# Later gates, unsplit value products, wider down chunks and a merge whose state-space branch runs one chunk behind, in a two-layer diffusion block on one Trainium2 core

## The chip, the core and the metric

The program runs on one core of a Trainium2 chip. TensorE (PE in the rows; its weight loads are PEld) multiplies matrices into PSUM, VectorE (DVE) and ScalarE (ACT) work on SBUF and PSUM, and SyncE (SP) issues nearly all loads. Each engine runs its own instructions in a fixed order and waits at semaphores for the others. The metric is the time of one execution on the device in microseconds (us), as the median of a few runs.

## The reference

```python
for l in range(2):                       # 256 context + 256 latent tokens, width 1024, FFN width 2816
    x  = ffn_half(x,  ml[0:3], g[0], ffn1)          # x + 0.5*gate*(silu(h@wg)*(h@wu))@wd
    xc = ffn_half(xc, mc[0:3], g[0], ffn1)          # the same weights for the context stream
    u, gq, gk, gv, nq, nk, nv, gates = split_in(modulate(rmsnorm(x)) @ w_in)
    y_ssm = s5_mixer(...)                           # state space, gelu, then t * sigmoid(t @ w_glu)
    y_gqa = window_gqa_latent(...)                  # 8 heads of 64, 2 key heads, sink logit
    y_na  = neighborhood_attn_latent(...)           # 8 heads, local window, relative bias
    m = sig(g_s)*(y_ssm@w_p_ssm) + sig(g_a)*(y_gqa@w_p_gqa) + sig(g_n)*(y_na@w_p_na)
    x = x + ml[5] * (m @ w_out)
    # the context stream goes through the same mixers and merge in layer 0 only
    x  = ffn_half(x, ml[6:9], g[2], ffn2)           # context too in layer 0 only
return rmsnorm(x, final_g)
```

All of it is float32.

## The kernel before

Activations lie transposed: eight chunks of 128 channels by 512 columns, context in columns 0 to 255 and latent in 256 to 511. A weight chunk is loaded into `raw`, ScalarE rounds it to `whi`, VectorE keeps the rest as `wlo` (`wload`, L73 to L80, three buffers of each in a pool that all weights share), and one product is three matmuls: `whi` with the rounded activation, `whi` with its rest, `wlo` with the rounded activation (`mm3`, L82 to L85). Those three lines stand in nearly every row.

A half-step FFN (`ffn`, L388) makes 22 hidden chunks (`mid`) in two halves of eleven and after each half sums them down (`down`, L406): eight output chunks `pd` of 33 matmuls. The first half runs over all 512 columns. The second runs over the context's 256 columns for all eight chunks and then, with the weights loaded again, over the latent's 256; under the latter the next stage's norm of the context is threaded (`then`, a generator that is advanced once a chunk from the third on). That is so in three of the four FFNs; the last one has the latent alone. At the end the next stage begins with products of the context's half (`by_stream`, tiles `pbs`) while the latent's norm is finished.

The mixer (`mixer`, L707) projects with `proj` (tiles `pp`), and in four rounds does one chunk of window attention (two heads) and one of neighbourhood attention. `attend` (L804) makes scores `sc`, softmax on VectorE and ScalarE, transposes `pt`, copies `ptb`, and in `values` (L797) the products `po`: for each key block j and each of two heads a matmul that fills half of the array's columns. Between the calls `fill` computes some of the 24 merge gates (`gate`, 24 matmuls into `pp`, a tanh into `th`) early and parks them in HBM: all of branch 2 from chunk 1 on in layer 0, of branches 1 and 2 in layer 1 (`ahead`). After the last attention come the gates 0, 1, 2 of chunk 0 (L994).

The merge splits the eleven chunks of branch outputs into `yh` and `yl`, runs the state-space unit's gated product (`pgl`, with gelu before and tanh behind), and then goes through eight output chunks, each with three branches (`pbr`: 9, 12 and 12 matmuls) whose weights are three loads of 384, 512 and 512 columns, each times its gate. Then `w_out` (`pwo`). In layer 1 all this is done for the latent alone, over 256 columns.

The order on every engine is made by a scheduler from the program order, the dependences and the free buffers; `tc.issue_after(x)` keeps what it encloses behind instruction x in that order.

Of the kernel before, what the change touches and what calls it, by code (L numbers as in the profile page):

```python
# [10 lines left out]
F32 = mybir.dt.float32  # L11
# [16 lines left out]
def body(tc, A):  # L28
# [359 lines left out]
    def ffn(tp, l, n, streams, hook, mids=None, before=None, then=None):  # L388
        i = 2 * n
        both = len(streams) == 2  # L390
        c0 = HALF * streams[0]
        early = []

        def unit(f, j):
            w, ps = early.pop() if early else wload(A["up"][l, n, f, j], 1024), bank("pgu")
            for k in range(KC):
                mm_k(ps[:, :T - c0], w, k, c0, T)
            hook(0.01 * (T - c0))
            return ps

        def up(f, *done):
            mids[f] = mid_tiles(tp)
            pg, pu = [*done, *(unit(f, j) for j in range(len(done), 2))]
            gate_up(tp, mids[f], pg, pu, c0, T)

        def down(half, a, b, between=None):  # L406
            N = b - a
            for m in range(KC):
                if between and m >= 2:
                    next(between, None)  # L410
                ps = bank("pd")
# [295 lines left out]
    def mixer(l):  # L707
# [89 lines left out]
        def values(nk_, ptb, vt, out):  # L797
            po = pa.tile([128, T], F32, name="po", tag="po")
            for j in range(nk_):
                for hf, r in enumerate(halves):  # L800
                    PE.matmul(po[r, :HALF], vt[:, j, r], ptb[hf][:, j], start=j == 0, stop=j == nk_ - 1)  # L801
            S.copy(out, po[:, :HALF])

        def attend(K, Q, vt, out, heads, bias):  # L804

            for s in streams:
# [3 lines left out]
                for b in range(2):  # L810
                    q0 = HALF * s + 128 * b
                    ps = [pa.tile([128, T], F32, name="sc", tag="sc", bufs=2) for hf in range(2)]
                    for hf in range(2):
                        for j in range(2):
                            PE.matmul(ps[hf][:, :128 * nk_], Q[:, hf, q0:q0 + 128], K[:, hf, j, :128 * nk_], start=j == 0, stop=j == 1)  # L815
# [183 lines left out]
        yh = gp.tile([128, 11, T], F32R, name="yh")  # L999
        yl = gp.tile([128, 11, T], F32R, name="yl")  # L1000
        nat = lambda x: x.rearrange("p (x t) -> p x t", t=8)
        ty = [yP[:, c, :, x0:].rearrange("p t x -> p x t") for c in range(3)]
        S.activation(yP[:, :, :, x0:].rearrange("p c t x -> p (c t) x"), yP[:, :, :, x0:].rearrange("p c t x -> p (c t) x"),
                     AF.Gelu_apprx_tanh)
        for c in range(3):
            split(nat(yh[:, c, c0:]), nat(yl[:, c, c0:]), ty[c])
        pgs = []
        for c in range(3):
            wh, wl = wload(A["wglu"][l, c], 384)
            ps = bank("pgl")  # L1010
            for k in range(3):
                w = slice(128 * k, 128 * k + 128)
                mm3(ps[:, :N], wh[:, w], wl[:, w], yh[:, k, c0:], yl[:, k, c0:], k == 0, k == 2)
            pgs.append(ps)
        for c in range(3):
            g = pgs[c][:, :N]
            S.activation(g, g, AF.Tanh, scale=0.5)
            V.scalar_tensor_tensor(ty[c], nat(g), 1.0, ty[c], op0=ALU.add, op1=ALU.mult)
            glu_last = split(nat(yh[:, c, c0:]), nat(yl[:, c, c0:]), ty[c], scale=0.5)
        for src, o in ((gq, 3), (nq, 7)):  # L1020
            for c in range(4):
                split(yh[:, o + c, c0:], yl[:, o + c, c0:], src[:, c, c0:])
        mh = gp.tile([128, KC, T], F32R, name="mgh")
        ml = gp.tile([128, KC, T], F32R, name="mgl")
        spans = ((0, 3), (3, 7), (7, 11))
        later = Filler([], 0.34)
        if l == 0:
# [4 lines left out]
            def ada_late():  # L1032
                for j in range(40, 64):
                    junk = p3.tile([128, D], F32, name="ajunk", tag="ajunk", bufs=1)
                    ada_chunk(rw[:, j % 2], sb, junk, 0, j)
                    if j % 8 == 7:
                        ada_bias(0, j // 8)
                    yield 2.4
            anchor[0] = glu_last
            later.gens.append([ada_late(), 0])  # L1040
        for m in range(KC):
            acc = gp.tile([128, T], F32, name="macc", tag="macc")
            for b, (k0, k1) in enumerate(spans):
                j = 3 * m + b
                th = ths[b] if m == 0 else gate_back(j) if j in ahead else gate(j)
                wh, wl = wload(A["wp"][l, m][:, 128 * k0:128 * k1], 128 * (k1 - k0))
                pp = p3.tile([128, T], F32, name="pbr", tag="pbr")
                for k in range(k0, k1):
                    w = slice(128 * (k - k0), 128 * (k - k0) + 128)
                    mm3(pp[:, :N], wh[:, w], wl[:, w], yh[:, k, c0:], yl[:, k, c0:], k == k0, k == k1 - 1)  # L1050
                if b == 0:
                    V.scalar_tensor_tensor(acc[:, :N], th[:, :N], 1.0, pp[:, :N], op0=ALU.add, op1=ALU.mult)
                else:
                    V.scalar_tensor_tensor(th[:, :N], th[:, :N], 1.0, pp[:, :N], op0=ALU.add, op1=ALU.mult)
                    V.tensor_add(acc[:, :N], acc[:, :N], th[:, :N])
                if m:
                    later(0.01 * N + 0.00125 * N * (k1 - k0))
            split(mh[:, m, c0:], ml[:, m, c0:], acc[:, :N])
# [4 lines left out]
        for s in streams:  # L1063
            a, b = HALF * s, HALF * s + HALF
            ctx_norm = norm(l, 2, 0, 2) if s and not last else iter(())
            for m in range(KC):
                if m >= 2:
                    next(ctx_norm, None)
                wh, wl = wload(A["wout"][l, m], 1024)
                ps = bank("pwo")  # L1070
                for k in range(KC):
                    w = slice(128 * k, 128 * k + 128)
                    mm3(ps[:, :HALF], wh[:, w], wl[:, w], mh[:, k, a:b], ml[:, k, a:b], k == 0, k == KC - 1)
                evac_x(m, ps, l, 1, a, b)
        norms_in(None, None)
        xs.close()
# [2 lines left out]
    for l in range(L):  # L1079
        with ExitStack() as fs:  # L1080
# [23 lines left out]

            def ctx_norm():
                hook.finish(ada)
                yield from norm(l, 1, 0, 2)

            norms_in(pt_, "po")
# [4 lines left out]
        with tc.tile_pool(name=f"fb{l}", bufs=1) as tp:  # L1114
            if l == 0:
                with tc.tile_pool(name="ada9", bufs=1) as ap, tc.tile_pool(name="jp9", bufs=1, space=PSUM) as jp:
# [5 lines left out]

                    def ctx_norm():
                        hook.finish()
                        yield from norm(1, 0, 0, 2)

                    ffn(tp, 0, 1, (0, 1), hook, None, lambda: hook.finish(gate), ctx_norm())
# [101 lines left out]
```

## Time and profile before

| | |
|---|---|
| time, median of 3 runs | 2228.49 us (2228.1 to 2230.19) |
| profiled execution | 2233.92 us, of which the span is 2232.1 us |
| TensorE busy | 2163.5 us (97%), 12750 matmuls |
| VectorE, ScalarE busy | 1643.0 us (74%), 944.7 us (42%) |
| DMA | 378.15 MB, mean 169 GB/s |
| chain that ended last | PE 78%, DVE 10%, DMA 6%, ACT 3% |

A matmul's shown duration holds its passage through the array, which overlaps with the next one's; what a stream of matmuls costs is read from the distance between starts. Stages in the trace: layer 0's first FFN to 427 us, its mixer to 726, merge and output product to 931; its second FFN to 1298; layer 1's first FFN to 1677, mixer to 1927, merge and output product to 2023, last FFN to 2220.

### The profile page before, as it was taken

What the parts mean: (1) busy time and instruction counts of PE and PEld (TensorE: products, weight loads), DVE (VectorE), ACT (ScalarE), POOL (GpSimd) and SP (SyncE); (2) the same over time, 40 slices, a digit from 0 to 9 for tenths busy, and PEclk for the clock granted to TensorE, in tenths of its full rate; (3) what the DMA queues carried; (4) which work ended last, traced back from release to release, by engine and by line L of the source; (5) the groups of instructions that cost most, each with busy time, mean ns of one, the idle gap of its engine ahead of it and who ended that gap; (6) DMA issues with size and microseconds to landing.
All of it is one profiled execution on the core that took longest, in us unless ns stands there. A gap on an engine that the chain in (4) does not pass through costs nothing.

```text
span 2232.1 us, 33671 instructions
## 1 busy us (share of the span) xinstructions
PE 2163.5 (97%) x12750; PEld 1861.3 (83%) x12750; DVE 1643.0 (74%) x3204; ACT 944.7 (42%) x1600; POOL 0.7 (0%) x6
## 2 busy tenths in 40 slices
PE   7999999999999999999999999999999999899997
PEld 5888889977777788988888998888898888788997
DVE  4897897767665888897777897687776766566555
ACT  3322334466556423422232543223355655544443
POOL 0000000000000000000000000000000000000000
PEclk8999999999999999999999999999999999999999
DMA  8535645643431656575665555555566453264564
GB/s 310 173 118 183 199 155 168 206 132 105 155 98 36 209 194 197 194 235 165 190 198 167 173 191 181 163 173 176 172 170 212 149 170 122 79 209 157 176 191 122
DMA packets 141627, 378.15 MB, mean 169 GB/s; under 512 B 30869, under 2 KB 38549, under 8 KB 141465
## 3 DMA queue, kind: packets, MB, share of 16 engines
q1 hardware_dynamic: 140880, 375.88, 52.0%
q8 instruction: 100, 1.64, 0.3%
q14 instruction: 63, 0.51, 0.1%
q10 hardware_dynamic: 584, 0.12, 0.0%
HBM read 346.45 MB, written 29.50 MB: 168 GB/s over the span
## 4 chain that ended last, share of the span: by engine, by line
PE 78%; DVE 10%; DMA 6%; ACT 3%; issue 2%; SPq 0%; ACTq 0%; DVEq 0%
PE pgu L83 11%; PE pgu L85 11%; PE pgu L84 11%; PE pd L83 5%; PE pd L84 5%; PE pd L85 5%; PE pp L83 4%; PE pp L84 4%; PE pp L85 4%; DVE wlo L79 3%; PE po L801 2%; PE pt L793 2%; PE sc L815 2%; DMA raw<-dn 1%; ACT whi L77 1%
## 5 line engine op out<-in xcount | busy, mean ns | idle before, releaser
L77 ACT ACTIVATE whi<-raw 128x1024 fp32r<-128x1024 f32 (+4 forms) x520 | 477.8, 920 | 957.8 <-issue 271.3
L79 DVE TENSOR_TENSOR wlo<-raw,whi 128x1024 fp32r<-128x1024 f32 (+4 forms) x520 | 544.1, 1048 | 276.8 <-ACT whi L77 273.4
L83 PE MATMUL pgu<-Hh,whi 128*128 128x512 f32 (+1 forms) x1360 | 493.7, 364 | 4.0 <-ACT Hh L159 2.7
L84 PE MATMUL pgu<-Hl,whi 128*128 128x512 f32 (+1 forms) x1360 | 493.2, 363 | 0.0
L85 PE MATMUL pgu<-Hh,wlo 128*128 128x512 f32 (+1 forms) x1360 | 492.8, 363 | 0.5 <-DVE wlo L79 0.5
L85 PE MATMUL pd<-mid,wlo 128*128 128x256 f32 (+1 forms) x968 | 304.1, 314 | 1.3 <-DVE wlo L79 1.2
L83 PE MATMUL pd<-mid,whi 128*128 128x256 f32 (+1 forms) x968 | 303.2, 313 | 0.0
L84 PE MATMUL pd<-mid,whi 128*128 128x256 f32 (+1 forms) x968 | 303.0, 313 | 0.0
L83 PEld LDWEIGHTS pgu<-Hh,whi 128*128 128x128 f32 x1360 | 257.4, 190 | 45.4 <-ACT Hh L159 4.4
L85 PEld LDWEIGHTS pgu<-Hh,wlo 128*128 128x128 f32 x1360 | 257.6, 189 | 40.6 <-DVE wlo L79 0.9
L84 PEld LDWEIGHTS pgu<-Hl,whi 128*128 128x128 f32 x1360 | 257.7, 190 | 39.7 <-DVE Hl L160 0.6
L178 DVE SCALAR_TENSOR_TENSOR ajunk<-araw,sb 128x1024 f32<-128x1024 f32 x208 | 255.6, 1229 | 3.7 <-DMA araw<-ada 1.1
L85 PE MATMUL pp<-Hh,wlo 128*128 128x512 f32 (+1 forms) x672 | 240.5, 358 | 3.5 <-DVE wlo L79 3.4
L83 PE MATMUL pp<-Hh,whi 128*128 128x512 f32 (+1 forms) x672 | 241.3, 359 | 1.7 <-ACT whi L77 1.3
L84 PE MATMUL pp<-Hl,whi 128*128 128x512 f32 (+1 forms) x672 | 240.0, 357 | 0.0
L85 PEld LDWEIGHTS pd<-mid,wlo 128*128 128x128 f32 x968 | 182.4, 188 | 14.2 <-DVE wlo L79 2.1
L83 PEld LDWEIGHTS pd<-mid,whi 128*128 128x128 f32 x968 | 182.5, 189 | 11.7
L84 PEld LDWEIGHTS pd<-mid,whi 128*128 128x128 f32 x968 | 182.2, 188 | 11.8
L85 PEld LDWEIGHTS pp<-Hh,wlo 128*128 128x128 f32 x672 | 129.4, 193 | 21.8 <-DVE wlo L79 4.5
L83 PEld LDWEIGHTS pp<-Hh,whi 128*128 128x128 f32 x672 | 129.6, 193 | 21.4 <-issue 3.8
L84 PEld LDWEIGHTS pp<-Hl,whi 128*128 128x128 f32 x672 | 129.6, 193 | 17.6 <-issue 3.1
L243 DVE TENSOR_TENSOR gact<-gact,pgu 128x512 f32<-128x512 f32 (+1 forms) x86 | 53.1, 617 | 73.4 <-PE pgu L85 73.2
(295 smaller groups left out, 2887.2 us busy)
## 6 DMA issues: line engine op xcount, KB each, us to landing
raw<-up SPq DMA_DIRECT2D x176, 512.0 KB, 4.2
araw<-ada SPq DMA_DIRECT2D x104, 512.0 KB, 3.5
raw<-win SPq DMA_DIRECT2D x90, 512.0 KB, 4.2
raw<-dn SPq DMA_DIRECT2D x88, 384.0 KB, 3.2
raw<-dn SPq DMA_DIRECT2D x88, 320.0 KB, 3.0
rw<-ada SPq DMA_DIRECT2D x24, 512.0 KB, 3.5
raw<-wout SPq DMA_DIRECT2D x24, 512.0 KB, 4.2
mid<-ada SPq DMA_DIRECT2D x32, 256.0 KB, 5.2
```

The source lines that it names most:

```text
L77: S.activation(hi[:, :n], raw[:, :n], AF.Copy)
L79: anchor[0] = V.tensor_sub(lo[:, :n], raw[:, :n], hi[:, :n].bitcast(F32)).ins
L83: PE.matmul(out, wh, ah, start=first, stop=False)
L84: PE.matmul(out, wh, al, start=False, stop=False)
L85: pe_anchor[0] = PE.matmul(out, wl, ah, start=False, stop=last).ins
L178: V.scalar_tensor_tensor(junk, raw, 1.0, sb[:, s], op0=ALU.mult, op1=ALU.mult, accum_out=mod[:, l, j, s:s + 1])
L243: V.tensor_mul(g[:, :N], g[:, :N], pu[:, :N])
L793: PE.transpose(pt[:, b], p[:, 128 * b:128 * b + 128], ident)
L801: PE.matmul(po[r, :HALF], vt[:, j, r], ptb[hf][:, j], start=j == 0, stop=j == nk_ - 1)
L815: PE.matmul(ps[hf][:, :128 * nk_], Q[:, hf, q0:q0 + 128], K[:, hf, j, :128 * nk_], start=j == 0, stop=j == 1)
```

## The change

1. `down` of the second half, in the three FFNs with both streams: chunks 0 to 3 run over 512 columns with one load of each weight, then chunks 4 to 7 over the context's columns and then over the latent's. The threaded norm starts with the first latent chunk (the generators got one `yield` more) and what is left of it is issued behind the last.
2. `values`: for each key block the second head's matmul is issued before the first's.
3. The gates 0, 1, 2 of chunk 0 may be issued only behind the last score matmuls of the last attention.
4. Layer 1 parks 11 gates instead of 14.
5. Merge: the two attention branches' weights of a chunk are one load of 1024 columns in buffers of their own (one set in layer 0, three in layer 1), the state-space branch is a load of 384 columns and is done after the next chunk's attention branches. The gated product of the state-space unit stands behind chunk 0's attention branches in program order, and the splits of the attention outputs ahead of it. `yh`, `yl`, `mh`, `ml` have only the columns in use. In layer 1 every second `w_out` chunk uses the new buffers.

```diff
-        def down(half, a, b, between=None):
+        def down(half, a, b, ms=range(KC), between=None):
-            for m in range(KC):
-                if between and m >= 2:
+            for turn, m in enumerate(ms):
+                if between and turn:
                     next(between, None)
...
             if both and half == 1:
-                down(half, 0, HALF)
-                down(half, HALF, T, then)
+                down(half, 0, T, range(4))
+                next(then)
+                down(half, 0, HALF, range(4, KC))
+                down(half, HALF, T, range(4, KC), then)
+                for _ in then:
+                    pass
...
         def values(nk_, ptb, vt, out):
-                for hf, r in enumerate(halves):
+                for hf, r in ((1, halves[1]), (0, halves[0])):
                     PE.matmul(po[r, :HALF], vt[:, j, r], ptb[hf][:, j], start=j == 0, stop=j == nk_ - 1)
...
-        ahead = [3 * m + b for m in range(1, KC) for b in ((1, 2) if last else (2,))]
+        ahead = [3 * m + b for m in range(1, KC) for b in ((1, 2) if last and m % 2 else (2,))]
...
-        ths = [gate(j) for j in range(3)]
+        ths = {}
+        for j, behind in ((1, scored[-3]), (2, scored[-2]), (0, scored[-1])):
+            with tc.issue_after(behind):
+                ths[j] = gate(j)
...
+        wm = xs.enter_context(tc.tile_pool(name=f"wm{l}", bufs=3 if last else 1))
...
+        def branch(m, b):
+            if b == 1:
+                accs[m] = gp.tile([128, N], F32, name="macc", tag="macc", bufs=2)
+                weights[m] = wload(A["wp"][l, m][:, 384:], 1024, wm, "m")
+            k0, k1 = spans[b]
+            j = 3 * m + b
+            th = ths[b] if m == 0 else gate_back(j) if j in ahead else gate(j)
+            wh, wl = weights[m] if b else wload(A["wp"][l, m][:, :384], 384)
...
+        branch(0, 1)
+        branch(0, 2)
+        glu_last = linear_unit()
...
+        for m in range(1, KC):
+            branch(m, 1)
+            branch(m, 2)
+            branch(m - 1, 0)
+        branch(KC - 1, 0)
...
-                wh, wl = wload(A["wout"][l, m], 1024)
+                wh, wl = wload(A["wout"][l, m], 1024, *((wm, "m") if last and m % 2 else ()))
```

Three places in the engines' order. First TensorE at the end of layer 0's last attention, at the value products `po` (`ptb` of the first head is read by the matmul that comes first in the program before). Before:

```order
L793 MATMUL pt_6736<-ident_70,pr_6732 128x128 x4
L801 MATMUL po_6742<-ptb_6676,vt_6547 64x256
L84 MATMUL pp_6824<-Hl_69,whi_6820 128x512
L85 MATMUL pp_6824<-Hh_68,wlo_6822 128x512
L801 MATMUL po_6742<-ptb_6677,vt_6547 64x256
L801 MATMUL po_6742<-ptb_6676,vt_6547 64x256
L801 MATMUL po_6742<-ptb_6677,vt_6547 64x256
```

Now:

```order
L85 MATMUL pp_6574<-Hh_68,wlo_6572 128x512
L83 MATMUL pp_6574<-Hh_68,whi_6570 128x512
L805 MATMUL po_6558<-ptb_6493,vt_6363 64x256
L805 MATMUL po_6558<-ptb_6492,vt_6363 64x256
L805 MATMUL po_6558<-ptb_6493,vt_6363 64x256
L805 MATMUL po_6558<-ptb_6492,vt_6363 64x256
L805 MATMUL po_6558<-ptb_6493,vt_6363 64x256
```

The lone first matmul and the gate's matmuls behind it are gone: all eight stand together. In the order before, 23 of the 24 calls of `values` are cut in this way, now none.

Second TensorE at the start of that same attention call, from the end of its query projection on (`sc` are scores, `pt` transposes, `pp_6758` and `pp_6791` gates of chunk 0). Before:

```order
L83 MATMUL pp_6758<-Hh_68,whi_6754 128x512
L815 MATMUL sc_6616<-K_6500,Q_6609 128x256 x2
L84 MATMUL pp_6758<-Hl_69,whi_6754 128x512
L85 MATMUL pp_6758<-Hh_68,wlo_6756 128x512
L83 MATMUL pp_6758<-Hh_68,whi_6754 128x512
L84 MATMUL pp_6758<-Hl_69,whi_6754 128x512
L85 MATMUL pp_6758<-Hh_68,wlo_6756 128x512
```

Now:

```order
L85 MATMUL pp_6400<-Hh_68,wlo_6398 128x512
L821 MATMUL sc_6432<-K_6316,Q_6425 128x256 x2
L821 MATMUL sc_6433<-K_6316,Q_6425 128x256 x2
L821 MATMUL sc_6458<-K_6316,Q_6425 128x256 x2
L821 MATMUL sc_6459<-K_6316,Q_6425 128x256
L797 MATMUL pt_6444<-ident_70,pr_6440 128x128 x2
L821 MATMUL sc_6459<-K_6316,Q_6425 128x256
L797 MATMUL pt_6454<-ident_70,pr_6450 128x128 x2
L821 MATMUL sc_6494<-K_6316,Q_6425 128x512 x2
L797 MATMUL pt_6470<-ident_70,pr_6466 128x128 x2
```

Before, gate matmuls stand ahead of the scores and between them: 51 from the end of the query projection to the end of the call's value products. Now no gate stands between the query projection and the context's value products, and 16 stand in the whole call; the other 56 of the three gates follow it, with chunk 0's two attention branches behind them.

Third VectorE at the end of layer 0's first FFN (`nh`, `Hl`: the context's norm applied; `wlo`: weights, those of 128x1024 for the mixer's first three products; `nacc`: the latent's sum of squares). Before:

```order
L160 SCALAR_TENSOR_TENSOR Hl_69<-nh_3867,mod_75,Hh_68 128x256
L165 SCALAR_TENSOR_TENSOR X_67<-pd_3816,coef_77,X_67 128x256
L79 TENSOR_TENSOR wlo_3900<-raw_3896,whi_3898 128x640
L109 TENSOR_TENSOR nacc_4019<-nacc_4019,nsq_4024 128x256
L79 TENSOR_TENSOR wlo_3923<-raw_3919,whi_3921 128x768
L109 TENSOR_TENSOR nacc_4019<-nacc_4019,nsq_4027 128x256
L79 TENSOR_TENSOR wlo_3947<-raw_3943,whi_3945 128x640
```

Now:

```order
L165 SCALAR_TENSOR_TENSOR X_67<-pd_3718,coef_77,X_67 128x256
L160 SCALAR_TENSOR_TENSOR Hl_69<-nh_3769,mod_75,Hh_68 128x256
L160 SCALAR_TENSOR_TENSOR Hl_69<-nh_3773,mod_75,Hh_68 128x256
L160 SCALAR_TENSOR_TENSOR Hl_69<-nh_3777,mod_75,Hh_68 128x256
L79 TENSOR_TENSOR wlo_3808<-raw_3804,whi_3806 128x1024
L109 TENSOR_TENSOR nacc_3835<-nacc_3835,nsq_3849 128x256
L79 TENSOR_TENSOR wlo_3877<-raw_3873,whi_3875 128x1024
```

The last of the context's `Hl` stood two chunks ahead of the last down chunk; now it stands behind the last one's (`pd_3718`), and the three weight rests of the next stage follow it.

## Rows read from the trace of the kernel before

**Rows 1.** Page: span; busy time, share and instructions of TensorE.
```profile
span 2232.1 us, 33671 instructions
PE 2163.5 (97%) x12750; PEld 1861.3 (83%) x12750; DVE 1643.0 (74%) x3204; ACT 944.7 (42%) x1600; POOL 0.7 (0%) x6
```

**Rows 2.** Stretches: us, busy of PE, PEld, DVE, ACT, POOL, then clock, DMA share, GB/s.
```profile
455.00:726.00 271.00, 265.01 (x1423) 199.95 (x1422) 178.90 (x441) 171.64 (x391) 0.00 (x0) 1.00 0.30 100
...
1700.00:1927.00 227.00, 220.32 (x1416) 188.67 (x1414) 148.47 (x310) 137.51 (x276) 0.00 (x0) 0.95 0.44 139
...
1945.00:1996.00 51.00, 47.14 (x377) 45.23 (x375) 32.16 (x65) 24.25 (x41) 0.00 (x0) 1.00 0.64 197
```

**Rows 3.** PE in order of time: start, us, line, op, tiles, shape, count. Value products.
```profile
485.42 0.65 PE L801 MATMUL po<-ptb,vt 128*64 128x256 f32 x2
...
717.95 0.65 PE L801 MATMUL po<-ptb,vt 128*64 128x256 f32 x2
718.52 0.50 PE L84 MATMUL pp<-Hl,whi 128*128 128x512 f32 x1
718.86 0.40 PE L85 MATMUL pp<-Hh,wlo 128*128 128x512 f32 x1
719.18 1.94 PE L801 MATMUL po<-ptb,vt 128*64 128x256 f32 x14
721.05 0.50 PE L83 MATMUL pp<-Hh,whi 128*128 128x512 f32 x1
...
1889.99 0.65 PE L801 MATMUL po<-ptb,vt 128*64 128x256 f32 x2
```

**Rows 4.** Stretches, down products alone: 256 columns, then 512 (columns as in rows 2).
```profile
360.20:400.80 40.60, 39.95 (x330) 39.33 (x329) 4.29 (x9) 1.00 0.71 222
1049.20:1110.80 61.60, 61.57 (x264) 49.36 (x263) 6.10 (x14) 1.00 0.60 187
```

**Rows 5.** TensorE's waits, 726 to 746: who for whom, us in total, times, longest.
```profile
PE pbr L84 <- DVE yl L92: 1.6, 3, 1.0
PE pbr L83 <- ACT yh L88: 1.6, 2, 0.9
```

**Rows 6.** TensorE's waits, 1908 to 1946.
```profile
PE pbr L83 <- ACT whi L77: 2.6, 2, 2.1
PE pp L85 <- DVE wlo L79: 1.6, 1, 1.6
PE pt L793 <- ACT ptb L794: 1.1, 1, 1.1
```

**Rows 7.** TensorE's waits, 1940 to 2022.
```profile
PE pp L85 <- DVE wlo L79: 3.4, 4, 1.6
PE pp L83 <- ACT whi L77: 1.3, 1, 1.3
```

**Rows 8.** TensorE's waits at the ends of three FFNs: 360:440, 1290:1310, 1670:1690.
```profile
PE nps L115 <- DVE zp L909: 3.1, 1, 3.1
...
PE nps L115 <- DVE asc L580: 0.9, 1, 0.9
...
PE nps L115 <- DVE zp L909: 1.6, 1, 1.6
```

**Rows 9.** VectorE in order of time at the first FFN's end.
```profile
417.87 0.48 DVE L160 SCALAR_TENSOR_TENSOR Hl<-nh,mod,Hh 128x256 fp32r<-128x256 f32 x1
...
424.98 1.23 DVE L79 TENSOR_TENSOR wlo<-raw,whi 128x1024 fp32r<-128x1024 f32 x1 [0.48 <-ACT whi L77]
```

**Rows 10.** ScalarE in order of time after layer 0's last query projection.
```profile
698.43 1.06 ACT L77 ACTIVATE whi<-raw 128x1024 fp32r<-128x1024 f32 x1 [4.72 <-PE pp L84]
...
699.99 1.28 ACT L1003 ACT_TABLE_LOAD   x1
...
704.70 0.47 ACT L785 ACTIVATE pr<-sc,st 128x256 f32<-128x256 f32 x1
```

**Rows 11.** TensorE, the longest stretch at the lower clock between 37 and 2221 us.
```profile
1846.40:1856.50 10.10, 10.10 (x49) 0.50 0.76 234
```

More of the change, by code (lines that the diff above doesn't have):

```diff
@@ L799, in values @@
             for j in range(nk_):
-                for hf, r in enumerate(halves):
+                for hf, r in ((1, halves[1]), (0, halves[0])):
                     PE.matmul(po[r, :HALF], vt[:, j, r], ptb[hf][:, j], start=j == 0, stop=j == nk_ - 1)
             S.copy(out, po[:, :HALF])
+        scored = []
         def attend(K, Q, vt, out, heads, bias):
@@ L814, in attend @@
                         for j in range(2):
-                            PE.matmul(ps[hf][:, :128 * nk_], Q[:, hf, q0:q0 + 128], K[:, hf, j, :128 * nk_], start=j == 0, stop=j == 1)
+                            scored.append(PE.matmul(ps[hf][:, :128 * nk_], Q[:, hf, q0:q0 + 128], K[:, hf, j, :128 * nk_],
+                                                    start=j == 0, stop=j == 1).ins)
                     for hf in range(2):
@@ L993, in mixer @@
         pump(9)
-        ths = [gate(j) for j in range(3)]
+        ths = {}
+        for j, behind in ((1, scored[-3]), (2, scored[-2]), (0, scored[-1])):
+            with tc.issue_after(behind):
+                ths[j] = gate(j)
         mi.close()
         gp = xs.enter_context(tc.tile_pool(name=f"mg{l}", bufs=1))
+        wm = xs.enter_context(tc.tile_pool(name=f"wm{l}", bufs=3 if last else 1))
         p3 = xs.enter_context(tc.tile_pool(name=f"p3{l}", bufs=3, space=PSUM))
-        yh = gp.tile([128, 11, T], F32R, name="yh")
-        yl = gp.tile([128, 11, T], F32R, name="yl")
+        yh = gp.tile([128, 11, N], F32R, name="yh")
+        yl = gp.tile([128, 11, N], F32R, name="yl")
+        for src, o in ((gq, 3), (nq, 7)):
+            for c in range(4):
+                split(yh[:, o + c], yl[:, o + c], src[:, c, c0:])
         nat = lambda x: x.rearrange("p (x t) -> p x t", t=8)
@@ L1005, in mixer, with linear_unit @@
         for c in range(3):
[L1006 to L1024, printed above, removed]
+            split(nat(yh[:, c]), nat(yl[:, c]), ty[c])
+        def linear_unit():
+            pgs = []
+            for c in range(3):
+                wh, wl = wload(A["wglu"][l, c], 384)
+                ps = bank("pgl")
+                for k in range(3):
+                    w = slice(128 * k, 128 * k + 128)
+                    mm3(ps[:, :N], wh[:, w], wl[:, w], yh[:, k], yl[:, k], k == 0, k == 2)
+                pgs.append(ps)
+            for c in range(3):
+                g = pgs[c][:, :N]
+                S.activation(g, g, AF.Tanh, scale=0.5)
+                V.scalar_tensor_tensor(ty[c], nat(g), 1.0, ty[c], op0=ALU.add, op1=ALU.mult)
+                glu_last = split(nat(yh[:, c]), nat(yl[:, c]), ty[c], scale=0.5)
+            return glu_last
+        mh = gp.tile([128, KC, N], F32R, name="mgh")
+        ml = gp.tile([128, KC, N], F32R, name="mgl")
         spans = ((0, 3), (3, 7), (7, 11))
@@ L1038, in ada_late @@
                     yield 2.4
+        accs, weights = {}, {}
+        def branch(m, b):
[6 more added lines that the diff above has]
+            wh, wl = weights[m] if b else wload(A["wp"][l, m][:, :384], 384)
+            w0 = 3 if b else 0
+            pp = p3.tile([128, T], F32, name="pbr", tag="pbr")
+            for k in range(k0, k1):
+                w = slice(128 * (k - w0), 128 * (k - w0) + 128)
+                mm3(pp[:, :N], wh[:, w], wl[:, w], yh[:, k], yl[:, k], k == k0, k == k1 - 1)
+            acc = accs[m]
+            if b == 1:
+                V.scalar_tensor_tensor(acc, th[:, :N], 1.0, pp[:, :N], op0=ALU.add, op1=ALU.mult)
+            else:
+                V.scalar_tensor_tensor(th[:, :N], th[:, :N], 1.0, pp[:, :N], op0=ALU.add, op1=ALU.mult)
+                V.tensor_add(acc, acc, th[:, :N])
+            if m:
+                later(0.01 * N + 0.00125 * N * (k1 - k0))
+            if b == 0:
+                split(mh[:, m], ml[:, m], acc)
@@ L1039, in mixer @@
+        branch(0, 1)
+        branch(0, 2)
+        glu_last = linear_unit()
+        if l == 0:
             anchor[0] = glu_last
             later.gens.append([ada_late(), 0])
[L1041 to L1058, printed above, removed]
@@ L1072, in mixer @@
                     w = slice(128 * k, 128 * k + 128)
-                    mm3(ps[:, :HALF], wh[:, w], wl[:, w], mh[:, k, a:b], ml[:, k, a:b], k == 0, k == KC - 1)
+                    mm3(ps[:, :HALF], wh[:, w], wl[:, w], mh[:, k, a - c0:b - c0], ml[:, k, a - c0:b - c0], k == 0, k == KC - 1)
                 evac_x(m, ps, l, 1, a, b)
@@ L1106, in ctx_norm @@
                 hook.finish(ada)
+                yield
                 yield from norm(l, 1, 0, 2)
@@ L1124, in ctx_norm @@
                         hook.finish()
+                        yield
                         yield from norm(1, 0, 0, 2)
```

## The prediction

> **What bounds the kernel now.** I read the page's head first: TensorE is busy for 2163.5 of 2232.1 us, VectorE for 74%, ScalarE for 42% [rows 1]. Then the stretches: in both attention stages TensorE is busy for 97 to 98% of the time, VectorE and ScalarE for 61 to 66% [rows 2]. So a matmul's place on TensorE that goes is time that goes, as long as no wait takes it. The reader is to see next that "busy" hides something: a shown matmul overlaps its successor, so I read the distances between starts in order of time [rows 3] and over stretches of one kind of product [rows 4]. The waits come last, since TensorE has few: at the two joints of attention and merge [rows 5, 6], in layer 1's merge [rows 7] and at the ends of three FFNs [rows 8].
>
> **Part 2, value products.** In 23 of 24 calls a lone matmul (two rows, one for each half of the float32 product) is cut off from the rest, and gate matmuls run in the hole [rows 3] (the first starts at 485.42, the last at 1889.99). The lone one takes 717.95 to 718.52, 0.57 us. The two gate matmuls in the hole take 0.34 and 0.32 us where a product of 512 columns takes 0.233 in a stream [rows 4]: each turn from the half-width products to the full width, or back, costs about 0.1 us, and a cut call makes two turns more. The fourteen rows of the other seven take 719.18 to 721.05, 1.87 us, or 0.13 us a row against 0.29 in the lone pair: matmuls of the two heads run beside each other, and the seventh has no partner. The eighth becomes its partner now, since the pairs are formed in the order (second head, first head), which is the new order from the first matmul on. So 0.57 + 0.11 + 0.09 = 0.77 us a call, and 23 x 0.77 = 17.7 us. If the eighth cost another step of 0.21 us it would be 0.56 and 12.9 us. The short calls of layer 0's context have the same lone pair. All of it lies on TensorE, which the stage waits for [rows 2]; that the first matmul now waits for the second head's copy costs nothing where projections stand ahead of it, which they do in all calls but the last of each layer (below).
>
> **Part 1, down products.** A 256-column matmul takes 40.60/330 = 0.123 us, one of 512 columns 61.60/264 = 0.2333 us [rows 4]. Four chunks of 33 in three FFNs are 396 pairs: 396 x (2 x 0.123 - 0.2333) = 5.0 us. The 24 repeated weight loads with their splits go too; I cost them at nothing, as the split engines have room. *TensorE: Matmul & The Clock Gate* in the Trainium skill (Back-to-back issue gap) speaks against this size: a fixed 2.5 ns beside the columns, so a pair would save 2.5 ns and all of them 1.0 us. The trace does not agree, at 12.7 ns a pair, some of it weight waits; by the page the sum would be 4 us smaller.
>
> The price stands at the FFN's end. The context's norm is applied while the last three latent chunks run instead of six, so VectorE reaches the next stage's three weight rests and the latent's sum of squares about when its last `Hl` is done. Stepping through VectorE's new order with the durations of the old (0.48 us an apply step, 1.23 a 1024-column rest [rows 9]), the latent's sum is ready some 7 us after the last down matmul, where the old one shows 3.1, 0.9 and 1.6 us of wait before that same product [rows 8]; but nine more products stand ahead of it now. I take 0 for the three ends together, between 4 us lost (the weight rests late at each) and 4 gained (the waits of rows 8 all but gone).
>
> **Part 3, the gates held back, layer 0.** Before, 51 gate matmuls of 0.23 us fill the last call, from the release of the weight split at 698.43 [rows 10] to the end of the value products at 721.05 [rows 3]: 22.6 us. The softmax chain sets that length and stays: weight split, queries, table load, gelu, queries, table load, and the first exponential 6.3 us after the release [rows 10], then eight softmaxes one behind the other. Now 16 gate matmuls stand in it, 35 fewer: 35 x 0.23 = 8.0 us in which TensorE waits. Against that, 56 gate matmuls and 24 of the attention branches, 18 us, stand behind the call, under which ScalarE and VectorE make the state-space unit's operands: the 3.2 us of rows 5 go, and the chain runs perhaps 0.8 us quicker with nothing between its transposes. 8.0 - 3.2 - 0.8 = 4.0 us lost; between 8 lost and 3 gained (the waits go and the chain shrinks as much as the fill).
>
> **Part 3, layer 1.** Here all 72 gate matmuls (0.12 us) were used up before the last value products, and TensorE then waited 2.6, 1.6 and 1.1 us and some tenths [rows 6]. Now 49 stand in the call and 23 behind it. New waits: none of them may run ahead of the third score product, so TensorE waits for the queries behind a 1024-column split and rest, and for the release of a score tile by the first exponential, about 3 and 2 us; two later exponentials stand behind table loads or splits, 1 us each. That is as much as goes: 0, between 5 lost and 5 gained.
>
> **Parts 4 and 5.** TensorE's work is the same: three gates move from the attention to the merge. In layer 1's merge TensorE waits 3.4 and 1.3 us for weights [rows 7] at 197 GB/s [rows 2]. One load fewer a chunk, buffers of their own and 24 more matmuls (2.9 us) at every second chunk give loads time to land: 2.5 us gained, between 0 and 6. In layer 0 the single set of buffers adds a wait on ScalarE: the next chunk's split waits for the last attention product of this one, and behind it stand the splits of the gates. Between that product and the next chunk's first stand two gates and a branch of 9, 57 matmuls or 13 us, ten times a split: nothing.
>
> **Sum.** 17.7 + 5.0 + 0 - 4.0 + 0 + 2.5 = 21.2 us. The profiled execution took 2233.9 us, 1.8 around its span; 2233.9 - 21.2 = 2212.7. Its time lies 5.4 us above the median of the runs, so the median I expect is 2207.3, said as 2207.
>
> **Rivals.** *The joints cost nothing* (0.18). The held gates fill behind the calls and the chains shorten, so layer 0 gains 3 instead of losing 4, layer 1 gains 5, and the merge 4: 2207 - 13.5 = 2194. For it: the waits of rows 5 and 6 have their cover now. Against it: the order shows nothing to run in the first part of both calls.
>
> *The value products were not the bound* (0.11). If the softmax chain, and not TensorE, sets the attention's pace, TensorE waits for what it saves: 2207 + 17.7 = 2225. For it: a score product needs a tile that an exponential frees. Against it: VectorE and ScalarE at 61 to 66% with TensorE at 97 to 98% [rows 2].
>
> *The clock falls where TensorE is thinned* (0.07). The records show only 1.2 and 2.4 GHz, and spells of 0.50 behind stretches of small products or waits, the longest 10.1 us [rows 11], worth half their length. The two last calls are 22 and 20 us, now with 8 and 7 us of waits; if both ran at the lower level, with the first 10 us behind each and a spell of 4 us at each FFN's end, that is 74 us more, 37 us lost, if no chain hid any: 2244. It decides from 42 us more of lower clock on. The page named above (What's actually happening) says that the low level is the default and recent activity releases it, which is what this needs; against it, TensorE waited some 5 us at layer 1's joint before [rows 6] and that stage as a whole still shows 0.95 [rows 2].
>
> Forecast 0.64. No change means within 0.2%, 2224 to 2233, about what a measurement of this kernel can tell. Faster: nearly all of the forecast and the first rival, a fifth of the second: 0.83; same 0.11; slower 0.06. The forecast's own spread is about 9 us to either side from the bounds above; with the second rival's edge the range is 2193 to 2225.
>
> **What would show it.** Value products in 24 whole groups, a long one of 16 rows in about 1.9 us, with no turns in between. Down products of 132 matmuls in 31 us at the head of three second halves. TensorE idle about 8 us in layer 0's last attention call and none between the value products and the state-space unit. `nps` at the FFN ends no later than now. Layer 1's merge with under 3 us of waits for `wlo`. The forecast is wrong if sixteen rows take 2.1 us or more, if score products in mid-attention begin to wait for exponentials, or if the lower clock lasts much longer than before.

## The result, and the profile after

The changed kernel takes 2206.31 us (median of 4, 2205.09 to 2207.19) against 2229.34 us for the kernel before on the same chip: ratio 0.9891, 95% interval 0.9877 to 0.9904. The profiled execution took 2205.09 us.

The page's head, the rows that answer to [rows 1]:

```profile
span 2203.3 us, 32637 instructions
...
PE 2146.9 (97%) x12354; PEld 1838.6 (83%) x12354; DVE 1621.1 (74%) x3164; ACT 922.6 (42%) x1560; POOL 0.7 (0%) x6
```

TensorE lost 396 instructions and 16.6 us of busy time; the span lost 28.8, more than the 23.0 of the medians, since the profiled execution of before lay 4.6 us above its median and that of the changed kernel 1.2 below. Stretches that answer to [rows 2]: attention in layer 0, in layer 1, and layer 1's merge (columns as there):

```profile
455.00:703.50 248.50, 238.78 (x1337) 182.53 (x1335) 169.82 (x430) 161.54 (x372) 0.00 (x0) 0.98 0.32 103
1692.00:1899.50 207.50, 199.78 (x1279) 170.64 (x1277) 144.72 (x310) 132.96 (x268) 0.00 (x0) 0.92 0.41 128
1919.00:1968.00 49.00, 49.00 (x411) 49.00 (x411) 36.07 (x59) 24.05 (x36) 0.00 (x0) 1.00 0.67 222
```

The merge is full now, at 222 GB/s (47.14 of 51.00 at 197 before). Both attention stages are less full than before (96% against 97 to 98%), and layer 1's runs at a mean clock of 0.92 where it was 0.95: something was paid there.

TensorE in order of time at layer 0's last value products, which answers to [rows 3]:

```profile
701.32 0.40 PE L83 MATMUL pp<-Hh,whi 128*128 128x512 f32 x1
701.64 1.95 PE L805 MATMUL po<-ptb,vt 128*64 128x256 f32 x16
703.52 0.50 PE L84 MATMUL pp<-Hl,whi 128*128 128x512 f32 x1
```

All 24 calls stand whole, and sixteen rows take 701.64 to 703.52, 1.88 us. The down products of 512 columns in the first FFN's second half ([rows 4]):

```profile
359.30:390.10 30.80, 30.79 (x132) 24.78 (x132) 2.61 (x6) 1.00 0.55 173
```

30.80/132 is 0.2333 us, as in the stream before.

### The profile page after: what moved, and what is told of

It reads as the page before. It is cut to its first block, busy times and chain, and to the rows that moved or that the text cites. A ratio compares the mean times of both kernels' runs of the same rounds, so it can differ in the third digit from the quotient of the medians.

```text
span 2203.3 us, 32637 instructions
## 1 busy us (share of the span) xinstructions
PE 2146.9 (97%) x12354; PEld 1838.6 (83%) x12354; DVE 1621.1 (74%) x3164; ACT 922.6 (42%) x1560; POOL 0.7 (0%) x6
## 5 line engine op out<-in xcount | busy, mean ns | idle before, releaser
L77 ACT ACTIVATE whi<-raw 128x1024 fp32r<-128x1024 f32 (+2 forms) x480 | 455.6, 950 | 950.7 <-issue 318.3
L79 DVE TENSOR_TENSOR wlo<-raw,whi 128x1024 fp32r<-128x1024 f32 (+2 forms) x480 | 520.8, 1087 | 275.0 <-ACT whi L77 273.1
L83 PE MATMUL pd<-mid,whi 128*128 128x256 f32 (+1 forms) x836 | 281.1, 336 | 0.0
L84 PE MATMUL pd<-mid,whi 128*128 128x256 f32 (+1 forms) x836 | 280.5, 336 | 0.0
L85 PE MATMUL pd<-mid,wlo 128*128 128x256 f32 (+1 forms) x836 | 280.4, 335 | 0.0
L84 PEld LDWEIGHTS pd<-mid,whi 128*128 128x128 f32 x836 | 157.4, 188 | 17.8
L83 PEld LDWEIGHTS pd<-mid,whi 128*128 128x128 f32 x836 | 157.4, 188 | 17.8
L85 PEld LDWEIGHTS pd<-mid,wlo 128*128 128x128 f32 x836 | 157.3, 188 | 17.8
L84 PEld LDWEIGHTS pp<-Hl,whi 128*128 128x128 f32 x672 | 129.9, 193 | 17.1 <-issue 2.3
```

The costliest lines, as they stand in the source:

```text
L77: S.activation(hi[:, :n], raw[:, :n], AF.Copy)
L79: anchor[0] = V.tensor_sub(lo[:, :n], raw[:, :n], hi[:, :n].bitcast(F32)).ins
L83: PE.matmul(out, wh, ah, start=first, stop=False)
L84: PE.matmul(out, wh, al, start=False, stop=False)
L85: pe_anchor[0] = PE.matmul(out, wl, ah, start=False, stop=last).ins
```

## The experiments

Each kernel stands against the kernel before, timed on the same chip in turn with it. "Mixer" is the time from a layer's first state-space projection (`pbs`) to the first output projection (`pwo`) in the profile, and the last column is what the clock records show at 0.50 within layer 1's mixer. So the value products, the joint and the merge lie inside a mixer, the FFNs outside.

| kernel | median us (n) | ratio, interval | mixer 0 | mixer 1 | at 0.50 |
|---|---|---|---|---|---|
| before | 2229.34 (4) | 1 | 447.9 | 318.5 | 27.3 |
| changed | 2206.31 (4) | 0.9891, 0.9877 to 0.9904 | 436.9 | 307.8 | 34.1 |
| e1 | 2222.57 (12) | 0.9967, 0.9952 to 0.9982 | 451.4 | 311.4 | 23.9 |
| e2 | 2216.36 (6) | 0.9945, 0.9928 to 0.9962 | 435.9 | 319.1 | 44.4 |
| e3 | 2195.95 (4) | 0.9855, 0.9837 to 0.9873 | 433.8 | 304.8 | 27.3 |
| e4 | 2210.73 (6) | 0.9922, 0.9908 to 0.9937 | 435.7 | 309.7 | 41.0 |
| e5 | 2204.09 (4) | 0.9879, 0.9860 to 0.9898 | 433.7 | 307.3 | 23.9 |
| e6 | 2203.35 (4) | 0.9876, 0.9856 to 0.9896 | 431.5 | 309.0 | 27.3 |
| e7 | 2198.78 (4) | 0.9854, 0.9833 to 0.9874 | 433.8 | 305.5 | 27.3 |
| e8 | 2199.24 (4) | 0.9865, 0.9849 to 0.9880 | 437.1 | 303.4 | 23.9 |
| e9 | 2210.97 (4) | 0.9912, 0.9887 to 0.9937 | 441.0 | 312.1 | 27.3 |
| e10 | 2220.71 (5) | 0.9961, 0.9949 to 0.9973 | 446.6 | 309.4 | 20.5 |
| e11 | 2198.02 (4) | 0.9857, 0.9843 to 0.9871 | 431.6 | 306.5 | 30.7 |
| e12 | 2211.01 (6) | 0.9920, 0.9905 to 0.9936 | 433.7 | 314.2 | 23.9 |

Before itself gave medians of 2228.7, 2233.8 and 2229.3 us beside the three groups of experiments (e1 to e4; e5, e6, e7, e9; the rest), so the new kernels are compared by their own medians below. Two cautions go with that. The first group ran on one chip and the other two on another, and the executions of one kernel lie 2 to 5 us apart, those of e1, e2 and e12 even 8 to 12; so e7, e8 and e11, at 2 to 3 us from e3 and with intervals that overlap its own, are not clearly slower than e3. And the mixer columns come from one execution of each kernel.

**e1 and e2, the value products.** e1 undoes the edit in the changed kernel, e2 makes it alone in the kernel before.

```diff
-                for hf, r in ((1, halves[1]), (0, halves[0])):
+                for hf, r in enumerate(halves):
```

> The changed kernel with one edit undone: the value products are again written first head, second head. All 24 calls of values are then cut again (a lone product, then 7 or 3). My theory: each cut costs TensorE 0.77 us, which the attention stage waits for, so 24 x 0.77 = 18.5 us more than the changed kernel, about 2224.8 us; if the eighth pair had its own step of 0.21 us in the whole group, 24 x 0.56 = 13.4 us more, 2219.7. Rival, value products were not the bound (the softmax chain sets the pace and takes what TensorE saves): no change, 2206 us, with the saved time as waits of score products for exponentials in the changed kernel.

> The kernel before with one edit alone: the value products written second head, first head, so that all 24 calls stand whole; gates, down chunks and merge as before. My theory: 23 cuts of 0.77 us go and nothing else, 2229.3 - 17.7 = 2211.6 us. Rival, value products were not the bound: 2229 us. A third reading, that part of the gain of the whole change came through the joints: the gain here stays clearly under 17 us, say 10 to 14, while undoing it in the changed kernel costs more.

16.3 us slower, between the theory's two sizes, and 12.4 us faster than before, within the third reading's 10 to 14. TensorE in e1, a cut call:

```profile
714.87 0.65 PE L805 MATMUL po<-ptb,vt 128*64 128x256 f32 x2
715.44 0.50 PE L85 MATMUL pp<-Hh,wlo 128*128 128x512 f32 x1
715.78 0.40 PE L83 MATMUL pp<-Hh,whi 128*128 128x512 f32 x1
716.10 1.94 PE L805 MATMUL po<-ptb,vt 128*64 128x256 f32 x14
717.97 0.50 PE L84 MATMUL pp<-Hl,whi 128*128 128x512 f32 x1
```

714.87 to 717.97 is 3.10 us, less two gate products of 0.233 in a stream 2.63, against 1.88 whole: 0.75 us a call, as forecast. In mixer 0 the 16 calls are worth 14.5 us (e1) or 12.0 (e2, 16 cut before): all of it, 0.75 to 0.9 a call. In mixer 1 eight calls are worth 3.6 us in e1, and in the profiled execution of e2 seven are worth nothing. The rival "not the bound" falls; what layer 1 gives back stands under e12.

**e3, the gates free.**

```diff
-        ths = {}
-        for j, behind in ((1, scored[-3]), (2, scored[-2]), (0, scored[-1])):
-            with tc.issue_after(behind):
-                ths[j] = gate(j)
+        ths = [gate(j) for j in range(3)]
```

> The changed kernel with chunk 0's three gates free again, not held behind the last three score products. My theory: layer 0's last attention call has its fill back (8.0 us of waits go) and the 3.2 us of waits behind the call come back, with a chain 0.8 us longer: 4 us faster in layer 0, 0 in layer 1: 2202 us. Rival, holding the gates back pays: the waits at both joints come back (3.2 us in layer 0, 2.6 + 1.6 + 1.1 us in layer 1) and nothing is won in the calls, whose length the softmax chain sets, so 3 to 9 us slower, 2209 to 2215.

10.4 us faster than the changed kernel (8 by the ratios), at least twice what I expected; the intervals of the two ratios do not meet. The same stretch, layer 0's last call, in the changed kernel and then in e3:

```profile
680.64:703.50 22.86, 17.12 (x82) 10.94 (x80) 12.59 (x31) 15.38 (x31) 0.00 (x0) 0.78 0.07 20
```

```profile
680.64:703.50 22.86, 22.86 (x126) 17.04 (x124) 13.40 (x33) 16.99 (x35) 0.00 (x0) 1.00 0.19 52
```

With the gates held TensorE idles 5.7 us there and the clock falls; free, it is full. The waits of TensorE from layer 0's last query projection to the branches (675 to 745), changed and then e3:

```profile
PE sc L821 <- DVE Q L753: 4.7, 2, 2.9
PE sc L821 <- ACT pr L789: 0.4, 1, 0.4
```

```profile
PE pgl L83 <- ACT yh L88: 2.7, 1, 2.7
PE pgl L84 <- DVE yl L90: 0.4, 1, 0.4
```

So the wait behind the call does come back, 3.1 us, as the rival said, and is the smaller of the two: mixer 0 is 3.1 us shorter. In layer 1 the same waits, changed (1872 to 1925) and e3 (1866 to 1925):

```profile
PE sc L821 <- DVE Q L753: 2.6, 1, 2.6
PE sc L821 <- ACT pr L789: 1.0, 1, 1.0
PE pbr L83 <- ACT whi L77: 0.8, 1, 0.8
```

```profile
PE pp L83 <- ACT whi L77: 1.1, 1, 1.1
PE pp L85 <- DVE wlo L79: 0.8, 1, 0.8
```

The changed kernel has its new waits, but e3 has not got the 5.3 us of rows 6 back: mixer 1 is 3.0 us shorter. Something else had taken those waits away. Of the 10.4 us the two profiled executions show 8.5: 6.1 in the mixers, 1.5 in the third FFN, where only the changed kernel's records show 3.4 us at 0.50, 0.8 ahead of the first mixer, and under half a microsecond, up or down, in each other stage. Much of it may be the clock. All four executions of the changed kernel have a mean granted clock of 0.980 to 0.981, all four of e3 one of 0.985 to 0.986; between 37 us and the last down product the traces show 58 us at 0.50 in the changed kernel, 41 in e3 and 38 in before. At half their length the 17 us more are worth 8.5 us at most, less where TensorE had nothing to run (it is busy 17.12 of the 22.86 us above). The experiment shows what holding the gates costs, but does not part the waits from the clock.

**e4, the down chunks.** The changed kernel with this part as before:

```diff
-                down(half, 0, T, range(4))
-                next(then)
-                down(half, 0, HALF, range(4, KC))
-                down(half, HALF, T, range(4, KC), then)
+                down(half, 0, HALF)
+                down(half, HALF, T, then)
```

> The changed kernel with the down chunks of the three both-stream FFNs as before: all eight chunks per stream over 256 columns, the context's norm spread over six latent chunks. My theory: 396 products of 512 columns become 792 of 256, 12.7 ns more a pair, 5.0 us slower, 2211.3 us, with the FFN ends as they were. By the back-to-back gap of the Trainium skill (TensorE: Matmul & The Clock Gate), 2.5 ns a pair, 1.0 us slower, 2207.3. Rivals on the ends: where the denser end had lost 4 us, undoing it gives those back, 2207; where it had gained 4, 2215.

4.4 us slower; e12 below is e2 with the new down chunks and 5.4 us faster than it, though the intervals of those two meet. Both lie at my 5.0, but not by my price of 12.7 ns a pair. A stream of 256 columns without waits, in the changed kernel's last FFN (down products alone), and TensorE in e4's three second halves:

```profile
2159.00:2190.20 31.20, 31.20 (x263) 31.20 (x264) 3.39 (x7) 1.00 0.47 139
```

```profile
358.80:426.40 67.60, 65.34 (x537) 1.00 0.67 205
1216.70:1281.20 64.50, 64.34 (x538) 1.00 0.60 180
1599.50:1665.30 65.80, 64.60 (x537) 1.00 0.59 169
```

31.20/263 is 0.1186 us, so two such products cost 3.9 ns more than the 0.2333 of one with 512 columns: 1.5 us for 396 pairs. The same three stretches take 63.3, 63.3 and 63.1 us in the changed kernel, with TensorE never idle: 8.2 us less than in e4. Most of that is waits (3.6 us idle in e4, for weights and the norm) and uneven starts, which went with the repeated loads; other stages give part of it back (mixer 0 is 1.2 us longer in the changed kernel, and its third FFN has 3.4 us at 0.50). The Trainium skill (*TensorE: Matmul & The Clock Gate*, Back-to-back issue gap) gives its 2.5 ns for the gap of a matmul by itself and says that streams with weight loads are spaced otherwise; the 3.9 ns lie nearer to it than my 12.7, and the 4.4 us do not test it.

**e5 to e7, the merge.** e5 is e3 with the old merge (order, three loads, common buffers, 14 gates parked), e6 with the old loads and buffers, e7 with all 14 gates parked.

```diff
-            wh, wl = weights[m] if b else wload(A["wp"][l, m][:, :384], 384)
+            wh, wl = wload(A["wp"][l, m][:, 128 * k0:128 * k1], 128 * (k1 - k0))
```

> The kernel of e3 (gates free, 2196 us) with parts 4 and 5 undone: three loads a chunk from the common buffers, the linear unit ahead of all branches, chunks one behind the other, all 14 gates parked in layer 1. So it is the kernel before with new value products and new down chunks alone. As the prediction had it, parts 4 and 5 are worth 2.5 us: 2198.5 us. New theory, from what e1, e3 and e4 leave over of the 23 us: the merge's order and loads, not the held gates, took away the waits at both joints and in layer 1's merge (3.2 us of rows 5, 5.3 of rows 6, 4.7 of rows 7): about 12 us, 2208 us, with those waits back in the trace.

> The kernel of e3 with three loads a chunk from the common buffers again (384, 512, 512 columns); order of the merge and parked gates as in the changed kernel. Theory, loads and own buffers are what takes layer 1's merge waits (rows 7, 4.7 us): 3 to 5 us slower, 2199 to 2201 us, with waits for weights in layer 1's merge. Rival, the new order and the gates at every second chunk do it: no change, 2196 us.

> The kernel of e3 with all 14 gates of layer 1's merge parked again instead of 11; else as e3. Theory, the three gates in the merge give the weights time to land: without them the merge waits again, 1 to 3 us slower, 2197 to 2199 us. Rival, own buffers are enough: within 1 us of 2196 us, the three gates only change place.

8.1, 7.4 and 2.8 us slower than e3 by the medians; e7's ratio is that of e3. Layer 1's merge in e3 and then in e6, stretches that lie in the merge as 1919 to 1968 does in the changed kernel's, and TensorE's waits in e6 from 1894 to 1966:

```profile
1911.00:1960.00 49.00, 49.00 (x411) 49.00 (x410) 36.52 (x61) 24.08 (x37) 0.00 (x0) 1.00 0.68 217
1912.00:1961.00 49.00, 47.37 (x391) 46.58 (x390) 31.99 (x59) 23.12 (x40) 0.00 (x0) 1.00 0.63 199
```

```profile
PE pp L83 <- ACT whi L77: 1.8, 1, 1.8
PE pp L85 <- DVE wlo L79: 1.6, 3, 0.8
PE pbr L85 <- DVE wlo L79: 0.3, 1, 0.3
```

Full at 217 GB/s with the one load and its buffers, 47.37 of 49.00 at 199 without: in layer 1 the loads carry the merge's gain (mixer 1 +4.2, both with 27.3 us at 0.50), not the order. Of e7's 2.8 its mixer 1 shows 0.7, too little to decide between its two theories. My new theory for e5 got the size right and its place wrong: with the old order and free gates mixer 1 is only 2.5 us longer than e3's, and the waits of rows 6 are not back either. e5's profile is 7.0 us longer in all; where the other 4.5 come from is only partly seen (2.1 in the third FFN, again with 3.4 us at 0.50, and 1.4 behind layer 0's merge).

**e10 and e12, the size of the tiles.** What e5 and e2 differ in, beside the down chunks, is a line that I had read as mere tidying. e10 makes it alone in the kernel before, e12 undoes it in e5.

```diff
-        yh = gp.tile([128, 11, T], F32R, name="yh")
+        yh = gp.tile([128, 11, N], F32R, name="yh")
...
-        mh = gp.tile([128, KC, T], F32R, name="mgh")
+        mh = gp.tile([128, KC, N], F32R, name="mgh")
```

> The kernel before with one edit alone, for which the prediction had no term: the tiles of the merge's operands and sums (yh, yl, mgh, mgl, macc) hold the columns in use, in layer 1 256 instead of 512; everything else as before. New theory, from layer 1's mixer in e5 (307.3 us) and e2 (319.1 us): the smaller tiles no longer lie where the last attention call still works, so the linear unit's operands and products start inside that call, the waits at layer 1's joint go (5.3 us of rows 6) and layer 1's mixer takes 6 to 11 us less than the 318.5 of before: about 2221 us. Rival, the size of a tile changes nothing on the engines: 2229 us, 318.5 us.

> The kernel of e5 (value products and down chunks new, 2204 us) with those tiles at 512 columns again in layer 1 and nothing else changed, so the kernel before with the new value products and down chunks alone. New theory: layer 1's mixer 6 to 11 us longer than e5's 307.3, 2211 us or a little more, the joint's waits back, as the sum of the two parts forecasts too (2229.3 - 13 - 5). Rival, sizes change nothing and e5 against e2 is the down chunks' doing: 2204 us.

8.6 us faster than before (mixer 1 309.4), and 6.9 us slower than e5 (314.2): the new theory holds on both sides. ScalarE in e10 behind layer 1's last query split, and in e12 at the call's end:

```profile
1905.27 0.36 ACT L748 ACTIVATE Q<-pp 64x256 fp32r<-64x256 f32 x1
1905.53 1.33 ACT L88 ACTIVATE yh<-gq 128x256 fp32r<-128x256 f32 x4
...
1912.91 0.67 ACT L88 ACTIVATE yh<-yP 128x256 fp32r<-128x256 f32 x1
```

```profile
1901.13 0.37 ACT L806 COPY nq<-po 128x256 f32<-128x256 f32 x1 [3.65 <-PE po L805]
1901.40 1.71 ACT L88 ACTIVATE yh<-yP 128x256 fp32r<-128x256 f32 x3
1903.02 1.32 ACT L88 ACTIVATE yh<-gq 128x256 fp32r<-128x256 f32 x4
```

With 512-column tiles no `yh` is written before the last call's `po` is copied out, though `gq` was complete long before; with 256 columns the operands are made inside the call. The 14 traces part in the same way: in before, e2 and e12, the three with 512 columns, layer 1's first `yh` comes behind the last copy of `po`, in the eleven others 16 to 20 us ahead of it. The code says why a size can do this (the merge's pool is opened where the attention's has been closed, and takes its memory over); which tile of the call lay in the way was not read. TensorE in e10 then has the unit's products to fill the chain's gaps, and no 1 us waits between its last transposes:

```profile
1916.80 0.39 PE L83 MATMUL pgl<-yh,whi 128*128 128x256 f32 x1
...
1918.08 0.65 PE L801 MATMUL po<-ptb,vt 128*64 128x256 f32 x2
...
1920.19 1.94 PE L801 MATMUL po<-ptb,vt 128*64 128x256 f32 x14
```

e12 has rows 6 back nearly to the tenth:

```profile
PE pbr L83 <- ACT whi L77: 2.6, 2, 2.1
PE pp L85 <- DVE wlo L79: 1.4, 3, 0.7
PE pt L797 <- ACT ptb L798: 1.1, 1, 1.1
```

e2 and e12 also show what became of layer 1's value products: against before, mixer 1 is 0.6 us longer in e2 and 4.3 us shorter in e12. From the state space's first product to the first output projection TensorE runs the same order in both, yet that takes 286.8 us in e2 and 282.3 in e12, with 41.0 and 23.9 us at the lower level. This need not be a difference of the two kernels: the profiled execution of e2 is the slowest of its six, that of e12 the fastest of its six. Over its six, e2 goes from 2220.5 us at a mean clock of 0.981 to 2212.4 at 0.985, and e12 from 2217.9 at 0.980 to 2208.3 at 0.986. At 0.985 before took 2226.8 to 2234.7 us beside e2 (four executions), 14 to 22 us more than e2's one at that clock, where I had forecast 17.7. So the clock takes part of the saving back, as far as one execution can say.

**e9, head by head.**

```diff
-            for j in range(nk_):
-                for hf, r in ((1, halves[1]), (0, halves[0])):
+            for hf, r in ((1, halves[1]), (0, halves[0])):
+                for j in range(nk_):
```

> The kernel of e3 with the value products written head by head: all chunks of the second head, then all of the first; each call still stands whole and computes the same. Theory behind 0.13 us a row and 0.77 us a cut call: products of the two heads write different halves of the 128 output rows and run beside each other, so a long call of 16 rows takes 1.9 us in pairs and about twice that head by head: 1.9 us x 16 + 0.95 us x 8 = 38 us slower, 2234 us. Rival, a product of this size takes 0.13 us by itself and the lone pair's 0.57 us is all turning: no change, 2196 us.

15.0 us slower than e3: the rival falls, and my size too.

```profile
708.62 2.86 PE L805 MATMUL po<-ptb,vt 128*64 128x256 f32 x16
711.41 0.50 PE L83 MATMUL pp<-Hh,whi 128*128 128x512 f32 x1
```

A long call takes 2.79 us instead of 1.88, not twice that: rows of one head start 0.216 us apart, but the first head's begin while three of the second's are still to come, and the short calls (1.02 us) lose nothing. 16 x 0.91 = 14.6 us, and both mixers grow by 7.2 and 7.3: here each microsecond of TensorE reaches the end.

**e8 and e11, versions to beat e3.** e8 issues layer 0's linear unit behind two branches; e11 has the single load in layer 1 alone.

```diff
-        glu_last = linear_unit()
+        with ExitStack() if last else tc.issue_after(pe_anchor[0]):
+            glu_last = linear_unit()
```

```diff
-        wm = xs.enter_context(tc.tile_pool(name=f"wm{l}", bufs=3 if last else 1))
+        wm = xs.enter_context(tc.tile_pool(name=f"wm{l}", bufs=3)) if last else None
```

> The kernel of e3 with layer 0's linear unit issued behind chunk 0's two attention branches, so that 21 branch products stand in front of the unit's. Theory: the waits at layer 0's joint in e3 (2.7 us for yh, 0.4 for yl, and 2 us of uneven starts) are covered: 2 to 4 us faster, 2192 to 2194 us. Rival, the branches wait in their place for the rests of the last attention output: 2196 us, no gain.

> The kernel of e3 with the single load and its own buffers in layer 1 only; layer 0 loads its three pieces into the common buffers again. Theory, from e6, whose layer 0 mixer took 431.5 us against 433.8 in e3 while its layer 1 mixer took 4.2 us more: in layer 0 the single set of buffers costs, so 2.3 us faster than e3, 2193.7 us. Rival, that difference was one execution's: 2196 us.

3.3 and 2.1 us slower than e3 by the medians, no gain in either, though not clearly a loss. In e8 TensorE waits at the same place for the branch's weights, longer than e3 waited for the unit's operands:

```profile
PE pbr L83 <- ACT whi L77: 5.6, 1, 5.6
```

In e11 mixer 0 is 2.2 us shorter, as its theory said, but mixer 1 is 1.7 and the third FFN 1.5 us longer, both with 3.4 us more at 0.50. e3 has the lowest median.

## Why the prediction was right, and where it was not

The time came out at 2206.3 where I said 2207, but not by its terms. The experiments make a ladder from before to the changed kernel: value products -12.9 (2229.3 to e2), down chunks -5.4 (to e12), tile sizes -6.9 (to e5), the merge -8.1 (to e3), gates held +10.4. My terms were -17.7, -5.0, none, -2.5 and +4.0. Two errors up and two down cancel, so that the total came within a microsecond is luck. The rungs are differences of medians; that from e2 to e12 is the weakest, since the executions of both scatter by 8 to 10 us.

*Value products, 17.7.* Right on TensorE (0.75 us a call against 0.77), right in layer 0, and e9 shows that TensorE bounds. The step that failed is that all of it reaches the time in layer 1 (4.3 us of 5.4 in e12, none in e2's profiled execution), because the clock does not stay where it was. Whole calls also move what stands beside them: in the first of layer 1's three state-space chunks 44 of 48 read-out products stand in one row, where before 16 and 32 stood apart. TensorE in the changed kernel:

```profile
1767.69 0.39 PE L85 MATMUL pp<-Hh,wlo 128*128 128x512 f32 x1
1767.92 0.30 PE L923 MATMUL py<-U,M 128*128 128x32 f32 x2
1768.06 0.61 PE L925 MATMUL py<-zp,WC 128*128 128x32 f32 x4
...
1771.86 0.62 PE L923 MATMUL py<-U,M 128*128 128x32 f32 x2
1772.28 1.04 PE L925 MATMUL py<-zp,WC 128*128 128x32 f32 x4
```

and the clock falls behind them:

```profile
1771.90:1782.10 10.20, 10.20 (x50) 10.20 (x50) 2.64 (x6) 2.12 (x4) 0.00 (x0) 0.50 0.70 195
```

All eleven kernels with whole calls show these 10.2 us there; before, e1 and e10, with cut ones, show 3.4 us or none. At half speed 10.2 us are worth up to 5 of the 6 us that eight calls save. But the spell alone does not settle the stage: e12 has it, and over the whole of mixer 1 shows 23.9 us at 0.50 against 27.3 in before. The row was not broken up in any run, so this cause is seen in step and not tested.

*Down chunks, 5.0, and FFN ends, 0.* Right in their sum, not in their price. The step that failed is reading 12.7 ns a pair as the cost of the products: without waits it is 3.9 ns, 1.5 us in all, and the rest is waits and uneven starts that went with the 24 repeated loads, which I had costed at nothing. Waits of TensorE at the first FFN's end (400 to 431):

```profile
PE pbs L83 <- ACT whi L77: 1.0, 1, 1.0
PE pbs L85 <- DVE wlo L79: 0.9, 1, 0.9
```

No `nps` waits, and the weights come late, as costed; the other two ends show the same pair at 1.9 and 2.0 us. 5.8 us in all stand where [rows 8] had 5.6.

*Held gates, layer 0, +4.0.* Right in mechanism (5.7 us idle, 8 forecast; the waits of rows 5 gone); mixer 0 lost 3.1. *Layer 1, 0.* Wrong: 3.0 lost. The step that failed is "as much goes as comes": I credited the held gates with the waits of rows 6, and the smaller tiles take those by themselves. The lower clock, which had no term, adds to both layers: all three kernels with held gates (changed, e1, e4) show 7 to 10 us at 0.50 in layer 0's last call, the free ones none before its end. This is the third rival's mechanism: 20 us more of lower clock than before up to the last down product, where that rival needed 42 to decide; the 17 us that e3 has less are up to 8.5 of its 10.4.

*Merge, layer 1, -2.5.* Right in kind (no `wlo` waits from 1919 to 1996, 222 GB/s), short in size: 4.2 in e6's mixer 1, 7 to 8 us over the whole kernel, partly unexplained. "Layer 0 nothing" was not: the single buffer set costs some 2.2 us of mixer 0 (e6 and e11).

*What had no term.* The tiles' sizes, 6.9 to 8.6 us. The diff showed them, and I read them only as memory.

Of the rivals, "joints cost nothing" gave 2194 for gates that fill behind the calls at no cost. e3 comes near that time by another way: it does not hold the gates, and TensorE still waits 3.1 us at layer 0's joint.

## What to carry to other kernels

A forecast that hits the total has not been tested until each part is run alone. A tile's size is a scheduling edit: where pools reuse memory, it decides when the next stage's first writes may start. Before work is held back to cover a later wait, ask whether the place that it leaves had other work, and try the kernel without the hold. And before two profiles are compared stage by stage, look where each lies among its kernel's own executions.

## What the runs showed of the hardware

Products into different halves of the output rows run beside each other even when they are not written in turn: TensorE began the second set with three of the first still to start, so 16 rows cost 2.79 us head by head and 1.88 in pairs. And an order does not fix where the clock falls: the six executions of e12 had mean granted clocks of 0.980 to 0.986 and took 2217.9 to 2208.3 us, and the profiled ones of e2 and e12, with the same TensorE order in layer 1's mixer, differed there by 4.5 us, with 17.1 us more at 1.2 GHz in the slower.
